# Rotated q rows of three latent head pairs: brought to their partitions by transfers on SyncE's queue instead of VectorE and ScalarE copies

## The chip, the cores and the metric

The kernel runs on one core of a Trainium2 chip. The metric is the device time of one execution in microseconds. Before the change three runs gave 741.9, 742.12 and 742.69 us (median 742.12). The profiled execution took 740.01 us, with a span of 738.2 us from its first to its last recorded instruction.

## The reference, cut to what matters

One encoder layer over 512 positions and a width of 1024: `h = x + Mixer(RMSNorm(x))`, `h = h + SwiGLU(RMSNorm(h))`, `y = RMSNorm(h)`. The mixer has eight forgetting-attention heads, eight latent-attention heads, two gates and an output projection. The change lies in the latent heads:

```
qb = (rms_norm(cq, q_a_norm_g) @ w_q_up).reshape(bsz, s_len, B_HEADS, B_NOPE + B_ROPE)
q_nope, q_rope = qb[..., :B_NOPE], qb[..., B_NOPE:]
q_rope = apply_rope(q_rope, cos[:, :, None, :], sin[:, :, None, :])
...
s = (jnp.einsum('bqhd,bkhd->bhqk', qn, k_nope, preferred_element_type=jnp.float32)
     + jnp.einsum('bqhr,bkr->bhqk', qr, k_rope, preferred_element_type=jnp.float32))
```

Each latent head has 64 plain and 32 rotary features; the rotary key is shared by all eight heads.

## The kernel before, in words

**Numbers as high and low parts.** Nearly every product is made three times on TensorE, high by high, high by low and low by high, in fp32r. The helper `split` (L101 to L105) makes the two parts: ScalarE writes the high part, VectorE subtracts it from the source and writes the low part. So every weight, every projection and every probability tile costs ScalarE and VectorE one pass each.

**Stages.** The input is loaded and split; the narrow projection is made; then come the up-projections of the latent heads, the attention over 64 items (8 latent heads, then 8 forgetting heads, 4 query blocks each), with the gate projections, the projections of the forgetting heads and the branch projections woven in between; then the output projection (L901), the SwiGLU and the final norm.

**Order of the work.** TensorE's instructions in the attention stage keep the order of the program text (`pin[0]`). The text weaves a list of filler jobs, `g12 c0 b1 g13 b2 g14 b3 g15 a0 v0 ...`, between the items: `g` is a gate projection, `b` a pair of latent heads (`project_b`), `c` the values, `a` a pair of forgetting heads (`project_a`). On VectorE, ScalarE, GpSimd and SyncE's queue the order is made by a planner that runs through the program with modelled times; each queue is then worked off strictly in that order. Tiles of the tag `u8` share 17 buffers, raw weights (`wraw`, tag `wr`) two; a load waits until the split of the load two before it has read its buffer.

**A pair of latent heads.** `project_b(j)` (L566) projects q and k of heads 2j and 2j+1 into PSUM (`pqb`, `pkb`). Each head has a tile `hd` (named `hb` in the profile) of four planes of 512 columns. Plane 3 holds, on partitions 0 to 99, what the rotary score product needs: high, low and again high rotated q (32 rows each) and four rows of the chunk mask. The rotated q of all heads stands in `qr4` (named `qr` in the profile), high and low, four heads to a plane, 32 rows each. Its rows are brought to partitions 0, 32 and 64 by L589 and L590 on VectorE and L591 on ScalarE. The mask rows come by L592 on GpSimd. The scores of an item (L643, tile `sp`) read planes 0, 1, 2 and 3. The first pair, j = 0, is made ahead of the attention loop; pairs 1 to 3 are fillers inside it. The buffer of `qr` is handed on to a head of the first forgetting pair (`ha`) once its last reader is done; GpSimd's L616 is the first to write there.

Of the kernel before, what the change touches and what calls it, by code (L numbers as in the profile page):

```python
# [8 lines left out]
F32 = mybir.dt.float32  # L9
# [57 lines left out]
def tile_hybrid_fox_mla_block(  # L67
# [6 lines left out]
    nc = tc.nc  # L74
# [11 lines left out]
    def u8(shape, dtype, name):  # L86
        return big.tile(shape, dtype, name=name, tag="u8", bufs=17)
# [7 lines left out]
    def bank(tag, name):  # L95
        return ps.tile([P, 512], F32, name=name, tag=tag, bufs=3 if tag == "a" else 5)

    def split(hi, lo, src, scale=None):

        if scale is None:  # L100
            one = nc.scalar.copy(out=hi, in_=src)  # L101
            two = nc.vector.tensor_tensor(out=lo, in0=src, in1=hi.bitcast(F32), op=ALU.subtract)  # L102
        else:
            one = nc.scalar.activation(out=hi, in_=src, func=AF.Copy, scale=scale)  # L104
            two = nc.vector.scalar_tensor_tensor(out=lo, in0=src, scalar=scale, in1=hi.bitcast(F32),  # L105
                                                 op0=ALU.mult, op1=ALU.subtract)
        if pin[1]:
            tc.keep_in_program_order(one)
            tc.keep_in_program_order(two)
# [14 lines left out]
    def mm3(o, a, b, start, stop):  # L124

        matmul(o, lhsT=a[0], rhs=b[0], start=start, stop=False)
        matmul(o, lhsT=a[0], rhs=b[1], start=False, stop=False)
        matmul(o, lhsT=a[1], rhs=b[0], start=False, stop=stop)
# [421 lines left out]
    def rotated_to_features():  # L550

        for g in range(2):
            pr = bank("b", "pr")
            for t in range(NT):
                transpose128(pr[:, t * P:(t + 1) * P], qrt[:, t * 256 + g * P:t * 256 + (g + 1) * P], ident)
            prs.append(pr)
        for g in range(2):
            split(qrh[g], qrl[g], prs[g], scale=SCALE_B)
# [3 lines left out]
    qrh, qrl = [qr4[:, g, :] for g in range(2)], [qr4[:, 2 + g, :] for g in range(2)]  # L562
# [3 lines left out]
    def project_b(j):  # L566

        cols = slice(j * P, (j + 1) * P)
        two = [u8([P, 4, S], F32R, f"hb{2 * j + e}") for e in range(2)]
        pq = bank("b" if j == 0 else "a", "pqb")  # L570
        for k in range(2):
            mm3(pq, (qn[:, 0, k, cols], qn[:, 1, k, cols]), (cq[:, 0, k, :], cq[:, 1, k, :]), k == 0, k == 1)
            yield
        pk_ = bank("b" if j == 0 else "a", "pkb")
        mm3(pk_, (kvs[:, 2, cols], kvs[:, 3, cols]), (kvs[:, 0, :], kvs[:, 1, :]), True, True)
        yield
        if j == 0:
            rotated_to_features()
        for e in range(2):
            h = 2 * j + e  # L580
            hd = two[e]
            own, oth = slice(64 * e, 64 * e + 64), slice(64 - 64 * e, 128 - 64 * e)
            split(hd[own, 0, :], hd[oth, 0, :], pq[own, :], scale=SCALE_B)

            nc.gpsimd.memset(hd[oth, 2, :].bitcast(F32), 0.0)
            split(hd[own, 1, :], hd[own, 2, :], pk_[own, :])
            nc.scalar.copy(out=hd[oth, 1, :], in_=pk_[own, :])
            rows = slice(h % 4 * ROPE, (h % 4 + 1) * ROPE)
            nc.vector.tensor_copy(out=hd[0:32, 3, :], in_=qrh[h // 4][rows, :])  # L589
            nc.vector.tensor_copy(out=hd[32:64, 3, :], in_=qrl[h // 4][rows, :])  # L590
            nc.scalar.copy(out=hd[64:96, 3, :], in_=qrh[h // 4][rows, :])  # L591
            nc.gpsimd.tensor_copy(out=hd[96:100, 3, :], in_=qrow)  # L592
            heads["b", h] = hd
            yield
# [138 lines left out]
    for _ in project_b(0):  # L733
        step()
# [74 lines left out]
    def job_of(job):  # L809
        n = int(job[1:])  # L810
        if job[0] == "b":
            return ("b", n), project_b(n), 5, 0.6
        if job[0] == "a":
            return ("a", n), project_a(n), 16, 0.64
        if job[0] == "c":
            return ("c", n), project_vb(), 4, 0.64
        if job[0] == "v":
            return ("v", n), project_va(n), 32, 0.32
        if job[0] == "g":
            return None, gates(n), 8, 0.64  # L820
        return None, branch("b", n, done_b), 8, 0.64
# [135 lines left out]
    for half in range(2):  # L957
# [27 lines left out]
        for t in range(NT):  # L985
# [18 lines left out]
            if half == 1:  # L1004
                r = mean_rsqrt([ssf[:, i:i + 1] for i in range(2 * t, 2 * t + (3 if t == NT - 1 else 2))], D, "nf")
                rows = slice(t * P, (t + 1) * P)
# [59 lines left out]
```

## Time and profile before

| | |
|---|---|
| median of 3 runs | 742.12 us (741.9 to 742.69) |
| profiled execution | 740.01 us, span 738.2 us |
| TensorE (PE) busy | 719.0 us, 97% of the span |
| VectorE (DVE) busy | 423.2 us, 57% |
| ScalarE (ACT) busy | 335.4 us, 45% |
| GpSimd (POOL) busy | 75.7 us, 10% |
| DMA | 69.45 MB, 94 GB/s on average |

Busy shares are averages over stages with different limits; the time line by stretches tells more. An engine name with a q at its end (SPq, PEq) is the engine's queue or sequencer, PEld is TensorE's loading of weights.

### The profile page before, as it was taken

To read this page: it belongs to the slowest core of one execution; us is meant where nothing else is said; L and a number is where in the kernel's file an instruction comes from. 1 tells how busy PE (TensorE), PEld (TensorE's weight loads), DVE (VectorE), ACT (ScalarE), POOL (GpSimd) and SP (SyncE) were. 2 spreads that over 40 slices of the span, in tenths; PEclk is the share of its full clock that TensorE was granted. 3 is DMA by queue.
4 is the path that set the end of the run, shared out by engine and by line. 5 is a ranking of instruction groups with operands and counts; after the bars stand their busy time and mean duration, and the time that the engine had idled before them with its cause. 6 is when DMAs were issued, how large, how long until landed. Compare 5 with 4: busy or idle time off the path is not lost.

```text
span 738.2 us, 9427 instructions
## 1 busy us (share of the span) xinstructions
PE 719.0 (97%) x3553; PEld 605.8 (82%) x3553; DVE 423.2 (57%) x819; ACT 335.4 (45%) x635; POOL 75.7 (10%) x96
## 2 busy tenths in 40 slices
PE   6999899999999999999999999999999999999996
PEld 4988778989888888887898888888888888888885
DVE  6998988777998985666733333233333233225215
ACT  7457978656684874434433223232232222213113
POOL 4243441021140121200000000000000000000000
PEclk9999999999999999999999999999999999999999
DMA  8512122131322222265303332332323323223212
GB/s 284 173 34 69 44 58 59 30 87 32 113 60 61 84 57 86 86 228 172 113 1 115 86 114 86 96 105 86 112 87 93 107 86 107 94 86 113 87 58 114
DMA packets 68941, 69.45 MB, mean 94 GB/s; under 512 B 3808, under 2 KB 58352, under 8 KB 68896
## 3 DMA queue, kind: packets, MB, share of 16 engines
q1 hardware_dynamic: 66240, 64.91, 29.6%
q10 hardware_dynamic: 1824, 3.38, 1.3%
q0 software_dynamic: 832, 0.57, 0.3%
q8 instruction: 28, 0.46, 0.3%
q14 instruction: 17, 0.14, 0.1%
HBM read 66.59 MB, written 2.10 MB: 93 GB/s over the span
## 4 chain that ended last, share of the span: by engine, by line
PE 87%; DVE 6%; ACT 2%; DMA 2%; issue 2%; SPq 0%; ACTq 0%; DVEq 0%
PE pg L115 26%; PE pu L115 16%; PE pd L115 16%; PE pqa L115 6%; PE pb L115 6%; PE po L115 4%; PE pva L115 3%; PE sp L115 3%; PE py L115 3%; PE pt L120 2%; DMA wraw<-in_w_out_dram 1%; DMA wraw<-in_w_in_dram 1%; PE ptr L120 0%; DVE wol L102 0%; ACT xTh L104 0%
## 5 line engine op out<-in xcount | busy, mean ns | idle before, releaser
L102 DVE TENSOR_TENSOR wlo<-wraw,whi 128x1024 fp32r<-128x1024 f32 x102 | 125.3, 1228 | 200.1 <-ACT whi L101 199.8
L101 ACT CAST whi<-wraw 128x1024 fp32r<-128x1024 f32 x102 | 106.8, 1048 | 211.0 <-PE pu L115 78.5
L115 PE MATMUL pd<-whi,act 128*128 128x512 f32 (+1 forms) x364 | 109.2, 382 | 0.0
L115 PEld LDWEIGHTS pd<-whi,act 128*128 128x128 f32 x364 | 67.6, 188 | 13.2
L115 PE MATMUL pg<-hTh,wlo 128*128 128x512 f32 (+1 forms) x192 | 71.4, 372 | 0.0
L115 PE MATMUL pu<-hTl,whi 128*128 128x512 f32 (+1 forms) x192 | 71.3, 371 | 0.0
L115 PE MATMUL pu<-hTh,whi 128*128 128x512 f32 (+1 forms) x192 | 71.3, 371 | 0.0
L115 PE MATMUL pu<-hTh,wlo 128*128 128x512 f32 (+1 forms) x192 | 71.3, 371 | 0.0
L115 PE MATMUL pg<-hTl,whi 128*128 128x512 f32 (+1 forms) x192 | 71.3, 371 | 0.0
L115 PE MATMUL pg<-hTh,whi 128*128 128x512 f32 (+1 forms) x192 | 71.1, 371 | 0.0
L115 PE MATMUL pd<-wlo,act 128*128 128x512 f32 (+1 forms) x182 | 69.5, 382 | 0.0
L115 PE MATMUL pg<-xTh,whi 128*128 128x512 f32 x128 | 52.4, 410 | 0.0
L115 PE MATMUL pg<-xTh,wlo 128*128 128x512 f32 x128 | 50.2, 392 | 0.0
L115 PE MATMUL pg<-xTl,whi 128*128 128x512 f32 x128 | 50.0, 391 | 0.0
L115 PEld LDWEIGHTS pu<-hTh,wlo 128*128 128x128 f32 x192 | 36.2, 188 | 6.3
L115 PEld LDWEIGHTS pg<-hTh,wlo 128*128 128x128 f32 x192 | 36.2, 188 | 6.3
L115 PEld LDWEIGHTS pg<-hTh,whi 128*128 128x128 f32 x192 | 36.2, 188 | 6.3
L115 PEld LDWEIGHTS pu<-hTh,whi 128*128 128x128 f32 x192 | 36.2, 188 | 6.2
L115 PEld LDWEIGHTS pu<-hTl,whi 128*128 128x128 f32 x192 | 36.2, 188 | 6.2
L115 PEld LDWEIGHTS pg<-hTl,whi 128*128 128x128 f32 x192 | 36.2, 188 | 6.2
L115 PEld LDWEIGHTS pd<-wlo,act 128*128 128x128 f32 x182 | 34.2, 188 | 6.7
L435 POOL TENSOR_SCALAR gate<-gate 128x512 f32<-128x512 f32 x16 | 27.4, 1714 | 115.9 <-ACT gate L433 108.6
(283 smaller groups left out, 1433.0 us busy)
## 6 DMA issues: line engine op xcount, KB each, us to landing
wraw<-in_w_in_dram SPq DMA_DIRECT2D x28, 512.0 KB, 3.9
wraw<-in_w_ffn_gate_dram SPq DMA_DIRECT2D x22, 512.0 KB, 3.7
wraw<-in_w_ffn_up_dram SPq DMA_DIRECT2D x22, 512.0 KB, 3.7
wraw<-in_w_ffn_down_dram SPq DMA_DIRECT2D x22, 512.0 KB, 3.7
wraw<-in_w_out_dram SPq DMA_DIRECT2D x8, 512.0 KB, 4.2
xf<-in_xT_dram SPq DMA_DIRECT2D x8, 256.0 KB, 5.6
wraw<-in_w_branch_b_dram SPq DMA_DIRECT2D x4, 512.0 KB, 3.5
wraw<-in_w_branch_a_dram SPq DMA_DIRECT2D x4, 512.0 KB, 3.4
```

Source lines behind the costliest of these rows:

```text
L101: one = nc.scalar.copy(out=hi, in_=src)
L102: two = nc.vector.tensor_tensor(out=lo, in0=src, in1=hi.bitcast(F32), op=ALU.subtract)
L115: ins = nc.tensor.matmul(*args, **kw)
L120: ins = nc.tensor.transpose(*args)
L435: nc.gpsimd.tensor_scalar(out=g, in0=g, scalar1=1e30, scalar2=None, op0=ALU.min)
```

## The change

For j = 1, 2 and 3 the three copies of rotated q rows into plane 3 are replaced by three transfers from SBUF to SBUF, issued on SyncE's queue: 32 rows of 2 KB each, 64 KB. The types are read as plain fp32 on both sides, so the bits are copied as they are. For j = 0 the copies stay. GpSimd's copy of the mask rows stays for all heads.

```
+            places = ((slice(0, 32), qrh), (slice(32, 64), qrl), (slice(64, 96), qrh))
+            if j:
+                for at, part in places:
+                    nc.sync.dma_start(out=hd[at, 3, :].bitcast(F32), in_=part[h // 4][rows, :].bitcast(F32))
+            else:
+                nc.vector.tensor_copy(out=hd[0:32, 3, :], in_=qrh[h // 4][rows, :])
+                nc.vector.tensor_copy(out=hd[32:64, 3, :], in_=qrl[h // 4][rows, :])
+                nc.scalar.copy(out=hd[64:96, 3, :], in_=qrh[h // 4][rows, :])
```

## Rows read from the trace of the kernel before

**Rows 1.** The page: TensorE's busy time, and the chain that ended last, by engine.
```profile
PE 719.0 (97%) x3553; PEld 605.8 (82%) x3553; DVE 423.2 (57%) x819; ACT 335.4 (45%) x635; POOL 75.7 (10%) x96
...
PE 87%; DVE 6%; ACT 2%; DMA 2%; issue 2%; SPq 0%; ACTq 0%; DVEq 0%
```

**Rows 2.** Stretches of 5 us, 40 to 120: busy PE, PEld, DVE, ACT, POOL; clock; DMA.
```profile
80.00:85.00 5.00, 5.00 (x24) 4.09 (x23) 4.88 (x10) 4.31 (x9) 1.72 (x3) 1.00 0.02 3
85.00:90.00 5.00, 2.96 (x16) 2.22 (x15) 4.81 (x14) 4.40 (x12) 1.04 (x2) 1.00 0.06 12
...
105.00:110.00 5.00, 3.87 (x17) 2.58 (x15) 4.83 (x10) 3.06 (x7) 3.04 (x5) 1.00 0.39 105
110.00:115.00 5.00, 4.35 (x25) 3.80 (x26) 4.84 (x11) 4.74 (x12) 0.47 (x1) 1.00 0.03 7
...
sum 80.00, PE 75.71 PEld 62.25 DVE 74.66 ACT 59.68 POOL 33.05; mean PE 4.73 PEld 3.89 DVE 4.67 ACT 3.73 POOL 2.07
```

**Rows 3.** TensorE's timeline, 60 to 120 us: the rows with idle time before them.
```profile
88.37 0.41 PE L120 MATMUL pt<-c,pe 128*128 128x128 f32 x2 [2.04 <-DVE pe L667]
...
107.48 0.70 PE L115 MATMUL sp<-hb 128*128 128x512 f32 x2 [0.91 <-DVE rs L666]
...
110.65 0.30 PE L120 MATMUL pt<-c,pe 128*128 128x128 f32 x1 [0.87 <-DVE pe L667]
```

**Rows 4.** The chain that ended last, 56 to 125 us: start, length, what.
```profile
75.53 0.41 DVE hb L589
...
84.75 0.15 DVE hb L590
...
87.97 0.27 DVE pe L667
...
104.39 0.73 DVE hb L590
```

**Rows 5.** Groups by line, 74 to 116 us, VectorE and then ScalarE: the copies.
```profile
L590 DVE CAST hb<-qr 32x512 fp32r<-32x512 f32 x6 | 3.8, 630 | 0.1
L589 DVE CAST hb<-qr 32x512 fp32r<-32x512 f32 x6 | 3.1, 520 | 0.2
...
L591 ACT CAST hb<-qr 32x512 fp32r<-32x512 f32 x6 | 3.7, 618 | 0.1
```

**Rows 6.** The same columns for a stretch of 20 us, later in the attention stage.
```profile
200.00:220.00 20.00, 20.00 (x107) 16.81 (x106) 19.12 (x49) 16.19 (x38) 7.68 (x10) 1.00 0.31 81
```

**Rows 7.** DMA issues by line: KB each, median us from issue to landing.
```profile
wraw<-in_w_in_dram SPq DMA_DIRECT2D x28, 512.0 KB, 3.9
...
krs<-c POOLq DMA_DIRECT2D x3, 16.0 KB, 1.9
```

**Rows 8.** SyncE's timeline: four loads of weights, start and length of the issue.
```profile
91.37 0.37 SPq L133 DMA_DIRECT2D wraw<-in_w_in_dram  x1
...
106.69 0.37 SPq L133 DMA_DIRECT2D wraw<-in_w_in_dram  x1
...
118.03 0.37 SPq L133 DMA_DIRECT2D wraw<-in_w_in_dram  x1
...
124.70 0.37 SPq L133 DMA_DIRECT2D wraw<-in_w_in_dram  x1
```

**Rows 9.** Timelines of four engines: first users of the loads, the new rows and `qr`'s buffer.
```profile
99.33 0.33 PE L115 MATMUL sp<-hb 128*128 128x128 f32 x2
...
102.25 0.52 POOL L585 MEMSET hb<- 64x512 f32 x1 [5.50 <-PE pqb L115]
...
108.43 0.52 POOL L616 MEMSET ha<- 6x512 f32 x1 [1.97 <-DVE hb L590]
...
115.47 1.05 ACT L101 CAST whi<-wraw 128x1024 fp32r<-128x1024 f32 x1
...
122.89 0.59 ACT L104 ACTIVATE ha<-pqa 64x512 fp32r<-64x512 f32 x1
```

**Rows 10.** Line 589's instructions: the semaphore instruction on VectorE's queue (ns min/median/max).
```profile
L589 DVEq EVENT_SEMAPHORE  x1: 21/21/21, 83.0 to 83.0; - x1
```

More of the change, by code (lines that the diff above doesn't have):

```diff
@@ L588, in project_b @@
             rows = slice(h % 4 * ROPE, (h % 4 + 1) * ROPE)
-            nc.vector.tensor_copy(out=hd[0:32, 3, :], in_=qrh[h // 4][rows, :])
-            nc.vector.tensor_copy(out=hd[32:64, 3, :], in_=qrl[h // 4][rows, :])
-            nc.scalar.copy(out=hd[64:96, 3, :], in_=qrh[h // 4][rows, :])
+            places = ((slice(0, 32), qrh), (slice(32, 64), qrl), (slice(64, 96), qrh))
[6 more added lines that the diff above has]
+                nc.scalar.copy(out=hd[64:96, 3, :], in_=qrh[h // 4][rows, :])
             nc.gpsimd.tensor_copy(out=hd[96:100, 3, :], in_=qrow)
```

## The prediction

> **What bounds the kernel now.** I read the page first. TensorE is busy for 97% of the span and the chain that ended last runs on it for 87%, with 6% on VectorE [rows 1]. So only work that makes TensorE wait is worth anything. The next view is the busy time by stretches around the pairs of latent heads [rows 2]. From 40 to 120 us TensorE is busy 75.71 of 80 us, so 4.29 us are idle, and nearly all of that sits in three stretches: 2.04 us from 85 to 90, 1.13 from 105 to 110, 0.65 from 110 to 115. VectorE is the full engine there, with 4.81 to 4.88 of 5 us, and 74.66 of the 80. TensorE's own timeline names what it waited for [rows 3]: 2.04 us for the scaled probabilities (L667), 0.91 us for a small VectorE operation (L666), which I read as a place in VectorE's queue, and 0.87 us for L667 again. Sum 3.82 us. All three waits end on VectorE. The third view is the chain between 56 and 125 us [rows 4]: from the first copy of rotated rows at 75.53 until L667 at 87.97 it never leaves VectorE, and the copies to be removed are links of it. Later, from 200 to 220 us, TensorE is busy for all of 20 us although VectorE is at 19.12 of 20 [rows 6]. So a VectorE that is nearly full does not stop TensorE by itself; what stops it is a burst in which a late item stands behind other work.
>
> **What is removed.** Pairs 1 to 3 are six heads. On VectorE go six L589 (3.1 us) and six L590 (3.8 us), together 6.9 us; on ScalarE six L591, 3.7 us [rows 5]. Whether they lie on the path must be taken stall by stall.
>
> The first stall, 2.04 us. Between 75.53 and 84.75 six copies are links of the chain; with the lengths that the chain gives them they are 0.41, 0.74, 0.45, 0.74, 0.41 and 0.15 us, 2.90 in all; the first and the last of the six are shown [rows 4]. L667 moves up by up to 2.90 us and was needed 2.04 us sooner [rows 3]. The stall goes, with 0.86 us to spare.
>
> The second stall, 0.91 us. Two more pairs of copies run between the two stalls, one of them ending with the copy at 104.39 in the chain shortly before [rows 4]. At the mean of a pair, 6.9 / 6 = 1.15 us [rows 5], the relief so far is 2.90 + 2.30 = 5.20 us, of which TensorE, being 2.04 us earlier, uses 2.04. What is left, 3.16 us, is more than 0.91. It goes.
>
> The third, 0.87 us. With the last pair the relief is some 6.4 us on this count, 6.9 by the groups [rows 5], against 2.04 + 0.91 + 0.87 = 3.82 us that TensorE can use. It goes too, unless something else is late next. Next in line would be ScalarE, which works 59.68 of the 80 us [rows 2] and itself loses 3.7 us [rows 5]; it follows VectorE in these stretches and has room.
>
> The gain is thus bounded by the idle time of TensorE: between 0, if other work moves into the freed places, and 4.29 us [rows 2]. I take 3.82, the three stalls.
>
> Here a rule of the Trainium skill can be set against the row. The rows of TensorE's busy time give 3.82 us. The Trainium skill, on its page "Perfetto Trace Analysis", section "Identifying the Most-Contended Engine", holds that matmul busy time misleads because matmuls are pipelined, and that the time in weight loads is the better measure. By it I compare the three stretches with the full one from 80 to 85 us: 4.09 less 2.22, less 2.58 and less 3.80 gives 1.87 + 1.51 + 0.29 = 3.67 us [rows 2]. The trace bears the busy times out here, and the sum by the rule would be 3.67 instead of 3.82.
>
> **What is added.** Eighteen transfers of 64 KB, three for each head, on SyncE's queue. The trace has no transfer of this kind. Its neighbours are 16 KB inside SBUF, 1.9 us from issue to landing, and 512 KB from memory, 3.9 us [rows 7]; 64 KB lies between, nearest to the 16 KB one, and I take 2.2 us. An issue takes 0.37 us [rows 8]; three make 1.1 us, six 2.2.
>
> Are they hidden? Head 2, the first to use a transferred row, is scored from 99.33 us [rows 9]; the copies of head 2 ran at 75.53 [rows 4]. That is 24 us for 1.1 + 2.2 us. Cost zero; without that cover, the transfer of a head would cost up to 1.1 + 3.9 = 5.0 us.
>
> The queue that they are moved past is SyncE's. A transfer waits there until its head's buffer is free. The latest are those of the last pair: GpSimd waited until about 102.2 us for that buffer, until the last projection `pqb` was done [rows 9]. Whatever stands behind them waits too, and that is a load of weights. The load issued at 91.37 us is the worst: behind six such transfers it would be issued at 102.2 + 2.2 = 104.4 and land by 108.7 with 0.4 us of the six on the same queue. Its reader (L101) starts at 115.47 [rows 8, 9]. So 7 us are left; with TensorE 3.8 us earlier some 3. Cost zero.
>
> Each score product of a new head waits for three landings more. That is a few short semaphore instructions on TensorE's sequencer; the trace of before shows none for these products, so I bound them by 0, if TensorE has work queued, and by 18 x 21 ns = 0.4 us, the length of such an instruction on VectorE's queue [rows 10]. I take the 0.4 off the gain, because these products are packed closely. VectorE and ScalarE lose nothing by the transfers, and GpSimd's copies stay.
>
> **The sum** against the profiled execution: 740.0 - 3.8 + 0.4 = 736.6 us. Later in the attention stage TensorE has no idle time [rows 6] and the chain follows it, and the loads of the output weights come after its last branch products, so an earlier TensorE stays earlier. The profiled execution is 2.1 us below the median of the runs shown. Moved to the median: 742.1 - 3.4 = 738.7 us.
>
> **The rivals.** First, a wait takes the place of the one removed: no change. VectorE's order is made anew by the planner, and the freed places can be filled by work that was behind (low parts of weights, low parts of heads), so that L667 comes as late as before. For it: VectorE keeps 74.66 - 6.9 = 67.8 of 76.2 us [rows 2, 5], 89%, and the margin of the first stall is 0.86 us. Against it: the copies are twelve of VectorE's instructions and the sum of its work really falls. Time: two of the stalls stay, 742.1 - 0.9, about 741.2 us; with all, 742.1.
>
> Second, slower, by the new place in SyncE's queue. `qr` is now released only when the last transfer has landed, and its buffer goes to the first forgetting pair, where GpSimd's L616 waited for the last copy until 108.43 and ScalarE writes at 122.89 [rows 9]. If the planner puts the last six transfers behind the load of 118.03, they land at 118.4 + 2.2 + 2.2 = 122.8: no harm. Behind that of 124.70 they land at 129.5 [rows 8], ScalarE stands for 6.6 us at the head of its queue, and the exponentials behind it with it. This decides as soon as they stand behind the load of 124.70, or of a later one. Time: 742.1 - 3.4 + 6.6 = 745.3 if nothing covers it, about 742 if half is covered. Against it: the buffers are free at 102.2, well ahead of the load at 106.69.
>
> Third, the planner's new order makes stalls elsewhere, most of all from 200 to 220 us, where VectorE has 0.88 us to spare in 20 [rows 6]. A stall costs 0.9 to 2.0 us [rows 3]; three or four would turn the gain round: 742.1 - 3.4 + 4 x 1.5 = 744.7 us. Nothing in the profile points to it except that full stretch.
>
> That the change doesn't do what it says can be left out: the transfers carry the same rows to the same places.
>
> **How the numbers follow.** About 0.2% (1.5 us) is what a measurement of this kernel can tell from no change. The forecast has 0.62, with a range of its own of 737.0 to 740.5. No change has 0.25: the first rival with 0.20, and 0.05 from the others where they only eat the gain. Slower has 0.13, about half of it for each of the other two rivals. The range goes from 737.0 (more than all of the 4.29 us idle gone, with the runs' own spread) to 743.2, which leaves out the worst of the slower cases and little at the low end.
>
> **What would show it.** In the profile of the changed kernel: no copy of `qr` after the first pair, eighteen transfers `hb<-qr` landing in 1.9 to 3.9 us; TensorE without the three stalls between 85 and 112 us; VectorE some 7 us less busy. A stall before `pt` or `sp` that is still there, now behind another line, is the first rival. ScalarE or GpSimd waiting for a transfer out of `qr` near 120 us is the second; new idle time of TensorE between 120 and 300 us is the third. The forecast is wrong if TensorE idles over 2.5 us between 60 and 300 us.

## The result, and the profile after

The changed kernel takes 735.04 us (median of 4 runs, 734.75 to 736.01); the kernel before, on the same chip, 742.01 us (4 runs, 740.59 to 742.69). The ratio is 0.9911, 95% interval 0.9893 to 0.9928. It is faster, as forecast, but by 7.0 us instead of 3.4, and below the range given.

The profiled execution took 734.85 us, with a span of 733.1 us against 738.2. From the page of the kernel after, the busy times and the chain that ended last, by engine:

```profile
PE 717.5 (98%) x3553; PEld 604.8 (83%) x3553; DVE 416.2 (57%) x807; ACT 331.6 (45%) x629; POOL 75.1 (10%) x96
...
PE 90%; DMA 3%; DVE 3%; ACT 2%; issue 1%; SPq 0%; ACTq 0%; DVEq 0%
```

VectorE loses 7.0 us and 12 instructions, ScalarE 3.8 us and 6, as counted ahead. VectorE's share of the chain falls from 6% to 3% [rows 1]. The stretches around the pairs, with the columns of [rows 2]:

```profile
80.00:85.00 5.00, 5.00 (x25) 4.08 (x24) 4.78 (x9) 4.40 (x11) 2.56 (x5) 1.00 0.28 62
85.00:90.00 5.00, 5.00 (x29) 4.26 (x29) 4.94 (x15) 4.75 (x15) 1.63 (x2) 1.00 0.11 13
105.00:110.00 5.00, 5.00 (x29) 4.25 (x28) 4.02 (x9) 3.85 (x10) 2.05 (x4) 1.00 0.40 109
110.00:115.00 5.00, 5.00 (x27) 4.23 (x26) 4.76 (x13) 4.37 (x11) 2.65 (x4) 1.00 0.29 72
```

TensorE has no idle time left where it had 2.04, 1.13 and 0.65 us. VectorE and ScalarE are still nearly full from 85 to 90 us; only what TensorE waits for is now done in time.

What stands against it is the transfers. The tile `hb` in the kernel after: the issues on SyncE (ns, least, median and most, first and last start), the landings; then GpSimd's first write to the buffer that `qr` had:

```profile
L593 SPq DMA_DIRECT2D hb<-qr x18: 507/588/1855, 75.2 to 102.5; - x18
...
DMA to landing us min/median/max: 1.9/2.9/4.4
...
105.39 0.52 POOL L622 MEMSET ha<- 6x512 f32 x1 [1.64 <-DMA hb<-qr]
```

The last of the eighteen is issued at 102.5 us, and `qr`'s buffer is free for its next user at 105.39, 3 us earlier than before [rows 9]. Head 2 is first scored at 96.64 us, 20 us after its transfers.

### The profile page after: what moved, and what is told of

It is laid out like the page before. It is cut to its first block, busy times and chain, and to the rows that moved or that the text cites. A ratio compares the mean times of both kernels' runs of the same rounds, so it can differ in the third digit from the quotient of the medians.

```text
span 733.1 us, 9449 instructions
## 1 busy us (share of the span) xinstructions
PE 717.5 (98%) x3553; PEld 604.8 (83%) x3553; DVE 416.2 (57%) x807; ACT 331.6 (45%) x629; POOL 75.1 (10%) x96
## 4 chain that ended last, share of the span: by engine, by line
PE 90%; DMA 3%; DVE 3%; ACT 2%; issue 1%; SPq 0%; ACTq 0%; DVEq 0%
PE pg L115 27%; PE pu L115 16%; PE pd L115 16%; PE pqa L115 6%; PE pb L115 6%; PE po L115 4%; PE sp L115 3%; PE pva L115 3%; PE py L115 3%; PE pt L120 2%; DMA wraw<-in_w_out_dram 1%; DMA wraw<-in_w_in_dram 1%; PE pqb L115 1%; PE ptr L120 0%; DVE wol L102 0%
```

## The experiments

### How much the kernel before varies, and where

No edit: the kernel before. Three more of its profiled executions follow further down.

> The kernel before, unchanged. The two profiled executions differ by 5.2 us (740.01 and 734.85), the medians by 7.0 (742.01 and 735.04); this run is to show where the other 1.8 us lie. Theory A (the stalls of the kernel before vary from execution to execution, because they come from a burst on VectorE): the median is again 741 to 742.5 us, and a profiled execution near that median shows stalls of TensorE between 85 and 112 us that sum to more than 3.8 us, up to 5.5 us. Theory B (the spread is elsewhere, in the first 60 us, where the granted clock falls): the stalls sum to 3.7 to 3.9 us as in the first profile, and the spans follow the granted clock.

Median 740.79 us (12 runs, 739.57 to 742.2), ratio to the other runs of before 0.9988 (0.9977 to 0.9998). Both sides are the same kernel, so an interval that just misses 1 is no difference yet. Its profiled execution took 741.04 us. The stalls are again 2.04, 0.87 and 0.85 us, so Theory A in its first form falls: the idle times do not vary. Nor did the first 60 us hold the excess over the first profile. It shows at the output weights, in TensorE's timeline of this run:

```profile
331.82 0.50 PE L115 MATMUL po<-wol,mgh 128*128 128x512 f32 x1 [0.30 <-DVE wol L102]
...
340.89 0.50 PE L115 MATMUL po<-woh,mgh 128*128 128x512 f32 x1 [1.30 <-DVE ha L911]
```

That is 1.60 us of waits, where the profile of before has one of 0.70. Against the first profile that costs 1.3 us from start to start of the products. So one part of the spread lies there, and it is not the change's.

### Each engine's copies alone

VectorE's two copies become transfers, ScalarE's stays:

```
             if j:
-                for at, part in places:
+                for at, part in places[:2]:
                     nc.sync.dma_start(...)
             else:
                 nc.vector.tensor_copy(...)
                 nc.vector.tensor_copy(...)
-                nc.scalar.copy(out=hd[64:96, 3, :], in_=qrh[h // 4][rows, :])
+            nc.scalar.copy(out=hd[64:96, 3, :], in_=qrh[h // 4][rows, :])
```

> Only the two VectorE copies of each of the six heads become transfers (12 of them); the ScalarE copy stays. Theory (the burst on VectorE is the cause): all three stalls go, 735 to 736 us, ratio to before 0.990 to 0.992. Rival 1 (ScalarE, relieved by 3.7 us, gave part of it): 736.5 to 739 us, with one of the three stalls left. Rival 2 (it is the planner's new order and not the time on VectorE): no prediction from the sums, anything from 734 to 743 us.

737.0 us, ratio 0.9937 (0.992 to 0.9953). That is 4.4 us of the gain, not all of it. TensorE's timeline has one stall left between 60 and 300 us, the first, cut from 2.04 to 1.16 us. Below it are rows of VectorE's and ScalarE's timelines of the same run:

```profile
88.93 0.41 PE L120 MATMUL pt<-c,pe 128*128 128x128 f32 x2 [1.16 <-DVE pe L672]
...
79.54 0.41 DVE L664 TENSOR_REDUCE nm<-sp 128x1 f32<-128x256 f32 x1
...
87.63 0.16 DVE L671 RECIPROCAL rs<-sm 128x1 f32<-128x1 f32 x1 [0.63 <-ACT pe L667]
...
80.56 0.62 ACT L596 CAST hb<-qr 32x512 fp32r<-32x512 f32 x1
...
85.78 0.62 ACT L596 CAST hb<-qr 32x512 fp32r<-32x512 f32 x1
86.43 0.58 ACT L587 CAST hb<-pkb 64x512 fp32r<-64x512 f32 x1
87.04 0.47 ACT L667 ACTIVATE pe<-sp,nm 128x256 f32<-128x256 f32 x1
```

The maximum of the item (L664) is ready at 79.95 us, and its exponential (L667 here) starts at 87.04. In the 7 us between them ScalarE works off other instructions, among them two of its copies of `qr` (80.56 and 85.78, 0.62 us each; a third runs at 78.82). VectorE then stands idle for 0.63 us until that exponential is done (L671). So with VectorE relieved it is ScalarE that brings the first stall, and Rival 1 holds. The planner's order has a part in it too: L587 at 86.43 stands ahead of the exponential here, and behind it in the kernel before. So some 0.6 us of the lateness may be the order's.

ScalarE's copy becomes a transfer, VectorE's two stay:

```
-            if j:
-                for at, part in places:
+            nc.vector.tensor_copy(out=hd[0:32, 3, :], in_=qrh[h // 4][rows, :])
+            nc.vector.tensor_copy(out=hd[32:64, 3, :], in_=qrl[h // 4][rows, :])
+            if j:
+                for at, part in places[2:]:
                     nc.sync.dma_start(...)
             else:
-                nc.vector.tensor_copy(...)
-                nc.vector.tensor_copy(...)
                 nc.scalar.copy(...)
```

> Only the ScalarE copy of each of the six heads becomes a transfer (6 of them); the two VectorE copies stay. Theory (VectorE): the stalls stay, 741 to 743 us, ratio 0.999 to 1.001. Rival 1 (ScalarE's part): 738 to 740 us. Rival 2 (the planner's order): anything from 734 to 743 us.

741.98 us, ratio 1.0005 (0.9993 to 1.0017). TensorE's stalls in its timeline:

```profile
89.38 0.41 PE L120 MATMUL pt<-c,pe 128*128 128x128 f32 x2 [2.05 <-DVE pe L672]
...
108.46 0.70 PE L115 MATMUL sp<-hb 128*128 128x512 f32 x2 [0.87 <-DVE rs L671]
...
112.09 0.30 PE L120 MATMUL pt<-c,pe 128*128 128x128 f32 x1 [1.33 <-DVE pe L672]
```

All three are there, as [rows 3] has them, the third somewhat longer. ScalarE's copies are worth nothing while VectorE's stand; once those are gone they are worth the rest, 0.9937 - 0.9911 = 0.26% or some 1.9 us. The intervals of the two ratios overlap; the stall that the run above still has costs 1.33 us from start to start of its products. The two parts do not add up: each alone gives 0.63% and nothing, together 0.89%.

### Copies and transfers both

```
-            if j:
+            nc.vector.tensor_copy(out=hd[0:32, 3, :], in_=qrh[h // 4][rows, :])
+            nc.vector.tensor_copy(out=hd[32:64, 3, :], in_=qrl[h // 4][rows, :])
+            nc.scalar.copy(out=hd[64:96, 3, :], in_=qrh[h // 4][rows, :])
+            if j:
                 for at, part in places:
                     nc.sync.dma_start(...)
-            else:
-                ...
```

> The copies of before stay for all heads, and the 18 transfers are made as well, to the same places after the copies. Theory (the gain is VectorE's time, the transfers are free): as before, 741 to 743 us, with the three stalls. If the transfers cost something on TensorE's path: 743 us or more. Rival 2 (the planner's order): anything from 734 to 743 us, without the three stalls although VectorE has all its copies.

741.29 us (12 runs), ratio 0.9998 (0.9981 to 1.0014). No cost and no gain of the transfers shows, to some 1.4 us either way. The stalls in the profile are 2.06, 0.91 and 0.84 us, although the planner ordered the work anew around the transfers: the gain is the time of the copies. But this execution shows more, in the stretches behind the first stall (the third column from the end is the granted clock):

```profile
85.00:90.00 5.00, 2.94 (x13) 2.17 (x12) 4.81 (x15) 4.36 (x12) 1.01 (x2) 0.87 0.22 51
90.00:95.00 5.00, 5.00 (x24) 4.24 (x23) 4.19 (x10) 3.76 (x10) 1.51 (x1) 0.79 0.37 105
```

After the stall that ends at 88.25 us TensorE ran for some microseconds at the lower of its two clocks, 1.2 GHz: products of 512 columns start every 0.43 us instead of 0.23. Matched product by product with the profile of before, that is some 1.5 us lost behind the stall, beside the idle time itself. I call it the stall's tail. In the profile that the prediction was made from, this did not happen.

### Each part of the pairs alone

```
-            if j:
+            if j == 1:
```

> Transfers for pair 1 alone (heads 2 and 3), copies for the others. Theory (each stall is worth what stands ahead of it on VectorE): the first stall falls from 2.04 us to 0 to 0.5 us, the second and the third stay, since pairs 2 and 3 keep their copies; 738 to 739.5 us, ratio 0.996 to 0.998. Rival (the planner's new order): stalls at other places.

738.84 us, ratio 0.9975 (0.9959 to 0.9991). TensorE's stalls:

```profile
86.32 0.41 PE L120 MATMUL pt<-c,pe 128*128 128x128 f32 x2 [0.79 <-DVE rs L672]
...
103.17 0.66 PE L120 MATMUL pt<-c,pe 128*128 128x128 f32 x4 [0.49 <-DVE yfb L702]
105.44 0.70 PE L115 MATMUL sp<-hb 128*128 128x512 f32 x2 [0.23 <-DVE ptl L102]
...
108.81 0.30 PE L120 MATMUL pt<-c,pe 128*128 128x128 f32 x1 [1.03 <-DVE pe L673]
```

The first falls to 0.79 us, less far than the 0 to 0.5 expected, the third stays, and the second is split in two: 0.49 + 0.23 us.

```
-            if j:
+            if j > 1:
```

> Transfers for pairs 2 and 3 (heads 4 to 7), copies for pairs 0 and 1. Theory: the first stall loses only the copies of head 4 that stood ahead of it and stays at 1 to 1.5 us; the second and the third go; 737.5 to 739 us, ratio 0.995 to 0.997. Rival (the planner's new order): stalls at other places.

737.16 us, ratio 0.9942 (0.9925 to 0.9959). One stall is left, the first:

```profile
87.48 0.41 PE L120 MATMUL pt<-c,pe 128*128 128x128 f32 x2 [1.23 <-DVE pe L673]
```

The second and the third went with the copies of pairs 2 and 3. Together the two kernels give 0.25% + 0.58% = 0.83%, near the 0.89% of the whole: each stall shrinks with the copies that stand ahead of it.

### The first pair by transfers too

```
-            if j:
+            if True:
```

> The first pair (heads 0 and 1) by transfers too, 24 in all. Its rows are ready only at 64 to 69 us and head 0 is scored at 72.1, so here the cover of the landing is thin. Theory (a landing of 1.9 to 4.4 us, issued one after the other behind a load, costs something only where its cover is short): TensorE waits 0 to 3 us for the scores of head 0, and the time is 735 to 738.5 us. Rival (the transfers cost nothing anywhere and VectorE's 2.5 us more are worth something): below 734.5 us.

735.92 us, ratio 0.9918 (0.9903 to 0.9933), no different from the change. TensorE waits nowhere between 60 and 300 us, though head 0 is scored from 72.2 us and its transfers are issued from 63.8. Their landings:

```profile
DMA to landing us min/median/max: 1.9/2.1/4.1
```

So even 8 us from issue to reader are cover enough here, and the VectorE time saved there is worth nothing, since TensorE did not wait for it.

### The changed kernel again

No edit.

> The changed kernel, unchanged, for its own spread beside that of the kernel before on the same chip. Matched product by product, the two profiled executions differ by 4.3 us at the three stalls (2.21, 1.08, 1.02), more than the 3.8 us of idle time shown, and the medians by 6.4 to 7.0. Theory (each of the lost stalls also sometimes brought a stretch at the lower granted clock, and that goes with the stall): the median is 735 to 736 us, the mean granted clock higher than that of the kernel before in the same job by 0.001 to 0.002 (0.7 to 1.5 us), and at equal granted clock the two differ by 4.5 to 5.5 us. Rival (the clock's stretches do not depend on the change): equal mean clocks, and a difference of the medians of 4.5 to 5.5 us.

735.44 us (4 runs), before 741.85 (10 runs), ratio 0.9914 (0.9899 to 0.9928): the first result again. The mean granted clocks of these runs are alike, 0.9925 and 0.9926, so the clock did not separate the two kernels here, as the rival has it; yet the medians differ by 6.4 us, more than the rival expects. So neither fits as a whole. Of 64 runs of the kernel before, on three chips (median 741.2), 31 have a granted clock of 0.992 or less, with a median of 741.7; the other 33 have 740.4. Of the 8 runs of the changed kernel (median 735.3) 2 have such a clock, at 736.0 and 736.35; the other 6 have a median of 735.1. Above 0.992 the two kernels are thus 5.3 us apart, within the theory's 4.5 to 5.5 us. But the mean clock of a run does not tell whether it had a tail: the run with both has one at a mean of 0.994, and the unedited run further up has none at 0.993.

### Three more profiled executions of the kernel before

> The kernel before once more, for another profiled execution. Of four executions with the whole first stall of 2.0 us, one so far shows a stretch at half the clock behind it (granted clock 0.87 and 0.79 in the two stretches of 5 us from 85 to 95, 1.4 us lost). Theory (this tail of the first stall, not the stall alone, is what the median of the kernel before holds over its fast executions): an execution near 740 us has no such stretch, one at 741.2 us or more has one of about 1.4 us, behind the first stall or behind the stall at 43.5 us. Rival (the spread has another source): an execution at 741.2 us or more with full clock from 42 to 118 us and its excess in other places.

739.84 us, full clock from 42 us on. 

> As the two looks before it: near 740 us with full clock from 42 to 118 us, or 741.2 us and more with a stretch at the lower clock there that accounts for the excess. Rival: an excess without such a stretch.

739.64 us, likewise. 

> As the look before it: near 740 us with full clock from 42 to 118 us, or 741.2 us and more with a stretch at the lower clock there that accounts for the excess. Rival: an excess without such a stretch.

741.48 us, and the stretch is there. The stretches of 5 us from 85 to 95, first of the execution at 741.48, then of that at 739.84:

```profile
85.00:90.00 5.00, 2.96 (x14) 2.17 (x13) 4.81 (x14) 4.40 (x12) 1.04 (x2) 0.90 0.07 12
90.00:95.00 5.00, 5.00 (x23) 4.20 (x22) 4.16 (x10) 3.75 (x11) 1.51 (x1) 0.76 0.39 105
```

```profile
85.00:90.00 5.00, 2.95 (x17) 2.23 (x17) 4.84 (x14) 4.39 (x14) 0.85 (x2) 1.00 0.05 8
90.00:95.00 5.00, 5.00 (x28) 4.26 (x28) 4.94 (x12) 4.78 (x12) 1.50 (x1) 1.00 0.39 108
```

The same stall of 2.04 us, with and without its tail; the matched products lose 1.55 us more with it, nearly the whole difference of 1.64 us between the two. Of seven profiled executions that have the whole first stall (the first one of the kernel before, four further ones of it, the run with both and the run with ScalarE's transfers), two show the tail. The three profiles without a first stall (the changed kernel twice and the one with four pairs) show none, nor do the three in which it is shortened to 0.79, 1.16 and 1.23 us. But the lower clock is not tied to the first stall. Near 43.5 us some executions of the kernels before and after alike wait some 1.3 us, at a place that the change doesn't touch, and two such executions (the runs with VectorE's and with ScalarE's transfers alone) have such a stretch behind it. Here the run with VectorE's transfers, then the unedited run further up, which waits there as long and keeps its clock:

```profile
45.00:50.00 5.00, 4.97 (x18) 4.01 (x19) 5.00 (x16) 0.69 (x2) 0.93 (x3) 0.66 0.34 89
```

```profile
45.00:50.00 5.00, 5.00 (x26) 3.96 (x26) 5.00 (x14) 1.13 (x3) 1.29 (x5) 1.00 0.41 104
```

### A version meant to beat both

In the changed kernel the row norms are called later:

```
     pin[0] = True
     ...
-    token_rms_rows()
     ...
     narrow(0, 2)
+    token_rms_rows()
```

> A version meant to beat both: the changed kernel with the row norms (L364 to L371) called after the first half of the narrow norms instead of ahead of them, so that VectorE's small products (L152, L153, 1.25 us for 128x4 numbers while GpSimd multiplies at L369) run ahead of GpSimd's two products. Theory (these small operations waited for GpSimd, and TensorE's stall of 1.3 us at 43.5 us came from it): the stall before ptc falls to 0.5 us or less, the stretch at the lower clock from 45 us no longer occurs, and the time is 733 to 734.5 us. Rival (the gates' rows are then late and TensorE waits for a PSUM bank instead): a new stall near 45 to 50 us, 735 to 737 us.

737.98 us, ratio to before 0.996 (0.9947 to 0.9972), where the change has 0.9911 and 0.9914: some 3 us slower than the change it was to improve. VectorE's small product, first in the kernel after, beside GpSimd's large one, then in this version:

```profile
39.80 1.37 POOL L369 TENSOR_TENSOR rm<-rm,rq 128x512 f32<-128x512 f32 x1 [14.62 <-DVE rot L305]
39.93 1.25 DVE L152 TENSOR_TENSOR mr_t<-mm,mr_q 128x4 f32<-128x4 f32 x1
```

```profile
39.13 0.15 DVE L152 TENSOR_TENSOR mr_t<-mm,mr_q 128x4 f32<-128x4 f32 x1
...
44.10 1.28 POOL L369 TENSOR_TENSOR rm<-rm,rq 128x512 f32<-128x512 f32 x1 [18.77 <-ACT rq L368]
...
52.79 1.28 PE L115 MATMUL pq<-upw,cq 128*128 128x256 f32 x6 [1.99 <-DVE kvs L102]
...
50.00:55.00 5.00, 3.01 (x16) 2.62 (x15) 5.00 (x20) 4.12 (x11) 3.11 (x2) 0.83 0.33 87
55.00:60.00 5.00, 5.00 (x27) 4.43 (x27) 3.21 (x16) 0.02 (x1) 0.00 (x0) 0.83 0.07 21
```

The cause of the small product's length is shown: ahead of GpSimd, which stands idle until 44.10, it takes 0.15 us instead of 1.25. The stall before `ptc` near 44 us is gone; of the two profiles of the changed kernel one has it with 1.32 and 0.45 us, the other with 0.44 alone. But a longer one of 1.99 us comes behind it, with a stretch at the lower clock after it; nine of its ten runs have a granted clock of 0.992 or less. So the theory fails. The rival was right in kind, though the time is above its 737 us: the wait moved to what is late next, a PSUM bank. `ptc` and `pq` share five, and the wait ended when VectorE had read the `ptc` tile into `kvs`. None of the versions run beats the change.

## Why the prediction was right in kind and too small

**What bounds the kernel: right.** Three waits of TensorE on VectorE, all gone; each went with the copies ahead of it, as the runs with pair 1 and with pairs 2 and 3 show.

**"L667 moves up by up to 2.90 us ... The stall goes, with 0.86 us to spare": wrong in its reason.** With VectorE's copies alone gone it moved only some 0.9 us against TensorE's products, and 1.16 us of the stall stayed. The chain of waits went through VectorE because VectorE was the later of two full engines. ScalarE was close behind, so "it follows VectorE in these stretches and has room" failed: the 59.68 of 80 us are an average, and in the stretches of the stall ScalarE was busy 4.31 and 4.40 of 5 us [rows 2]. The change took ScalarE's copies too, and so the stall went after all, but barely. The scaled probabilities for the product at the first stall, in the kernel before and then after:

```profile
87.88 0.35 DVE L667 TENSOR_SCALAR pe<-pe,rs 128x256 f32<-128x256 f32 x1
```

```profile
85.16 0.35 DVE L673 TENSOR_SCALAR pe<-pe,rs 128x256 f32<-128x256 f32 x1
```

Before, the product started 0.14 us after this operation ended. After, it started at 85.77, 0.26 us after the end: by my estimate from these rows some 0.1 us was to spare, not 0.86. That the whole stall went was in part luck.

**"I take 3.82, the three stalls": too small.** This is the term of the sum that failed, and with it the bound, "between 0 ... and 4.29 us", from which the low end of the range came. It failed twice over. First, idle time is not the whole cost of a stall. TensorE's timeline at the place of the first, the kernel before (its next row, at 88.37, stands in [rows 3]) and then after:

```profile
85.93 0.40 PE L115 MATMUL pg<-xTh,wlo 128*128 128x512 f32 x1
```

```profile
85.54 0.40 PE L115 MATMUL pg<-xTh,wlo 128*128 128x512 f32 x1
85.77 0.38 PE L120 MATMUL pt<-c,pe 128*128 128x128 f32 x2
```

After, the two products start 0.23 us apart; before, at 85.93 and 88.37, 2.44 us apart. The stall cost 2.21 us, of which 2.04 stood as idle time, because the product ahead of it counts as busy until its modelled end. The second and third cost 1.08 and 1.02 us against 0.91 and 0.87: in all 4.31 us. The sum by weight loads, 3.67 us, was farther off than the 3.82, so the trace bore out neither. Second, the first stall sometimes has a tail at the lower clock that costs some 1.5 us more, and the one profiled execution of before had none. The tail is seen in two of seven profiles and its share of all runs is not known; the granted clocks (31 of 64 runs low before, 2 of 8 after) can't give it, since they also count stretches elsewhere.

**"I take the 0.4 off the gain": wrong.** TensorE has no idle time at the new heads' scores; copies and transfers together cost as much as the copies alone. The term is 0.

**"Moved to the median: 742.1": too high.** Three runs stood for the kernel before. Over 64 the median is 741.2, 0.9 us below the median that the sum went to. Put together, 741.2 - 735.3 = 5.9 us, of which 4.3 are the stalls from start to start. The two profiled executions differ by 5.2 us: their first 78 us differ by 0.4 and the output weights by 0.1, which no part of the change explains, and from 78 to 120 us the matched products gain 4.6 us. What is left of the 5.9, some 1.6 us, fits the tails and the waits at the output weights, but was not split between them; that stays open. Side by side on one chip the two kernels differed by 7.0 and 6.4 us, so the open part may be up to 2.7. Against the pooled 735.3 the forecast of 738.7 missed by 3.4 us: 0.5 by the size of the stalls, 0.4 by the term for the landings, 0.9 by the median it started from, and the open 1.6.

**The cover of the transfers: right.** They take longer than said (median 2.9 us, up to 4.4, and 0.59 us for an issue instead of 0.37), and nothing waited for them on TensorE.

**The rivals.** No wait took the place of the ones removed, so the first falls. The second falls: the planner put the last transfers at 102.5 us, ahead of the load that it issues at 103.88. The third falls: TensorE has no idle time between 60 and 300 us.

## What to carry to other kernels

A stall on a chain through one full engine can be held by a second full engine right behind it; ask of each stall what the next late engine would give, read that engine's load in the stall's own stretch and not over 80 us, and move the work of both. Price a stall from start to start of the products around it, and ask what the clock does after it: a wait of 2 us of a busy TensorE cost 2.2 us here, and some 3.7 in two profiled executions. Copies that only move rows between partitions can leave full engines for a queue with slack, if their reader comes late enough: 8 us after the issue sufficed here.

## What was not expected of the hardware

The issue of a 64 KB transfer inside SBUF took SyncE 0.51 us or more (median 0.59), that of a load of 512 KB 0.37. TensorE dropped to its lower clock after a wait of 2.0 us in some executions and not in others of the same program, and in two executions already behind a wait of 1.3 to 1.4 us. And a product of 128x4 numbers on VectorE took 1.25 us while GpSimd multiplied 128x512 beside it, against 0.15 us with GpSimd idle. The Trainium skill, page "SBUF — State Buffer", section "Who interferes with whom", says that a VectorE instruction with two inputs in SBUF contends with a GpSimd instruction that reads SBUF; these two rows agree.
